# FFN weight units in halves and thirds, ring transfers that wait for their own bytes only, and new planning numbers, in an eight-core decoder step

## The chip, the cores and the metric

The kernel runs on all eight NeuronCores of one Trainium2 chip. Every core runs the same program on its own data: one prompt of 2048 tokens and four decode samples. The metric is the device time of the slowest core, in microseconds. Most executions of one kernel agree within a few tenths of a per cent, but some fall into a slower state, in which one die (four cores) or both run at a lower granted TensorE clock. A ratio below always compares fast runs with fast runs. The chips differ too: the fast runs of the kernel before had a median of about 2395 us where it was first timed and of 2404 to 2407 us on the later chips that had fast runs. So kernels are compared by their ratio to the kernel before in the same rounds, on the same chip.

## The reference, cut to what matters

```
for layer in range(2):
    x = x + 0.5 * swiglu_ffn(rmsnorm(x, ...), ffn_w_in[layer, 0], ffn_w_out[layer, 0])
    x = x + mixer(rmsnorm(x, ...))          # gated linear attention, then dilated window attention
    x = x + 0.5 * swiglu_ffn(rmsnorm(x, ...), ffn_w_in[layer, 1], ffn_w_out[layer, 1])

def swiglu_ffn(x, w_in, w_out):             # w_in 1024 x 5376, w_out 2688 x 1024
    g, u = jnp.split(x @ w_in, 2, axis=-1)
    return (jax.nn.silu(g) * u) @ w_out
```

Four FFNs make up most of the matrix work. Their weights are too large to stay on the core, so they are streamed from HBM once for each of four tiles of 512 tokens. The 32 sample tokens of a core share the loads of tile 0.

## The kernel before: the parts that matter here

The program is written by a small list scheduler. Tiles are Python generators that yield operations. The scheduler plans a start time for every operation from a cost model, and so fixes, before the run, the order of each engine's instructions and the semaphores between them. The plan decides nothing but order. Two tiles are in flight at a time, each with its own ring of weight buffers (12288 bf16 per partition).

```
class Sched:
    DMA_BW = 330e3        # planned rate, bytes of the float32 source per us
    DMA_LAT = 2.2         # planned time from a transfer's end to its landing
    ...
def ffn_units(f):
    for j in range(NF):                                   # 21 units: columns j of g and of u
        add_unit("fi%d" % f, j, wfi[f * NF + j], 2048)
    for m in range(8):                                    # 8 units: 128 output columns
        add_unit("fo%d" % f, m, wfo[f * 8 + m], 2688)

def weights(slot):                                        # one for each ring, issues on POOL
    for k, u in enumerate(order[slot]):
        # ... lo, hi: the next place in the ring; over: units whose bytes it covers
        yield need(lambda over=over: all(o.left == 0 for _, _, o in over))
        yield O(PL, (lambda e: e.dma_start(out=dst, in_=u.src)),
                writes=[u.key] + [o.key for _, _, o in over], cost=1.0, ...)

# in ffn(): a unit is waited for and released as a whole
u = yield from use(T, "fi%d" % f, j)
yield mm(g,  [(v[:, kt, 0:128],   T.h[:, kt, :]) for kt in range(8)], hks(T) + [u.key], ...)
yield mm(up, [(v[:, kt, 128:256], T.h[:, kt, :]) for kt in range(8)], hks(T) + [u.key], ...)
u.left -= 1
```

A load "writes" its own key and the key of every old unit that it covers. If it covers only a part of an old unit, the next load, which covers the rest, finds the first load as the last writer of that key. POOL then waits until the first load has landed before it issues the next, although the two share no byte. The loads narrow float32 to bfloat16 on the way, so 1 GB/s written is 2 GB/s read.

Of the kernel before, what the change touches and what calls it, by code (L numbers as in the profile page):

```python
# [24 lines left out]
class Sched:  # L25



    DMA_BW = 330e3
    DMA_LAT = 2.2  # L30

    def __init__(self, nc):
        self.nc = nc
# [277 lines left out]
def build():  # L311
# [128 lines left out]
    for t in range(4):  # L440
        def add_unit(kind, i, src, n, users=0, t=t):
            u = Unit(src, n, users or (1 if t else 2), (t, kind, i))
            u.kind = kind
            units[(t, kind, i)] = u
            order[t % 2].append(u)

        def ffn_units(f):
            for j in range(NF):
                add_unit("fi%d" % f, j, wfi[f * NF + j], 2048)
            for m in range(8):  # L450
                add_unit("fo%d" % f, m, wfo[f * 8 + m], 2688)
                if (t, f) == (3, 3) and m % 2 == 0:

                    order[0].append(order[1].pop())
        ffn_units(0)
        for gi, kind in enumerate(("v", "qk", "r", "o")):
            for i in range(4):
                add_unit(kind, i, wgl[gi * 4 + i], 2048)
            if t == 0 and kind == "qk":
                for s in range(4):  # L460
                    src = st_in[s * 4:(s + 1) * 4].rearrange("h p d -> p h d")
                    add_unit("S0", s, src, 2048, 1)
                    add_unit("S0b", s, None, 1024, 1)
        ffn_units(1)
        for i in range(2):
            add_unit("kv", i, wkv[i], 2048)
        ffn_units(2)
        for i in range(3):
            add_unit("wq", i, wqd[i], 2048)
        if t == 0:  # L470
            for s in range(4):
                add_unit("ck", s, ck[s], 3328, 1)
                add_unit("cv", s, cv[s], 3328, 1)
        for i in range(4):
            add_unit("wo", i, wod[i], 1536)
        ffn_units(3)
# [1 line left out]


    LEAD = 24 * 2048  # L480
    NWS = 8


    first = {(0, "fi0", 1): [("x", "b0", 5)]}
    for k in range(4):
        first[(1, "fi0", k)] = [units[(0, "fi0", 12 + 2 * k)].key]

    def weights(slot):
        ring = rings[slot]
        live = []  # L490
        off = 0
        yield need(lambda: S.lastw.get(("x", "b0", 7)) is not None)
        for k, u in enumerate(order[slot]):
            if off + u.n > RING or u.kind == "ck":
                off = 0
            lo, hi = off, off + u.n
            off = hi
            over = [(a, b, o) for (a, b, o) in live if a < hi and b > lo]
            yield need(lambda over=over: all(o.left == 0 for _, _, o in over))
            live = [x for x in live if x not in over] + [(lo, hi, u)] + [(a, lo, o) for a, b, o in over if a < lo] \  # L500
                + [(hi, b, o) for a, b, o in over if b > hi]
            u.ap = ring[:, lo:hi]
            if u.uid in first:
                yield need(lambda: all(k in S.lastw for k in first[u.uid]))
            dst = u.ap
            if u.kind == "S0":
                dst = dst.bitcast(F32).rearrange("p (h d) -> p h d", h=4)
            if u.src is None:
                u.keys = [u.key] + [o.key for _, _, o in over]
                u.ready = True  # L510
                continue
            yield O(PL, (lambda e, u=u, dst=dst: e.dma_start(out=dst, in_=u.src)),  # L512
                    first.get(u.uid, []), writes=[u.key] + [o.key for _, _, o in over], cost=1.0, dma="w%d_%d" % (slot, k % NWS), nbytes=u.n * 512)
            u.ready = True

    def use(T, kind, i):
# [124 lines left out]
    def load_x(T, prev):  # L641
        nq = 4 if T.n == 512 else 1
        for q in range(nq):
            ms = range(q * 8 // nq, (q + 1) * 8 // nq)
            if prev is not None:
                yield need(lambda: all(("y", prev.nm, m) in done for m in ms))
            if T.t == 1:
                after = units[(0, "fi0", 3 + 2 * q)]
                yield need(lambda: after.ready)
            w = len(ms) * T.n  # L650
            src = xp[T.t] if T.n == 512 else xs
            yield O(SP, (lambda e, q=q, w=w, src=src, ms=ms: e.dma_start(
                out=T.x[:, ms[0]:ms[-1] + 1, :].rearrange("p m n -> p (m n)"), in_=src[:, q * w:(q + 1) * w])),
                [after.key] if T.t == 1 else [], writes=[xk(T, m) for m in ms], cost=0.1, dma="x%s_%d" % (T.b, q), nbytes=w * 512)
        for m in range(8):
            yield from square(T, m)
# [66 lines left out]
    def hks(T):  # L723
        return [hk(T, m) for m in range(8)]
# [7 lines left out]
    def ffn(T, f, last):  # L732
# [12 lines left out]
            done.add(("act", T.nm, f, j))  # L745

        for j in range(NF):
            u = yield from use(T, "fi%d" % f, j)
            v = u.ap.rearrange("p (kt c) -> p kt c", kt=8)
            if n == 512:  # L750
                bs = yield from get_banks(2)
                g, up = PS[bs[0]], PS[bs[1]]
            else:
                bs = yield from get_banks(1)
                g, up = PS[bs[0]][:, 0:n], PS[bs[0]][:, n:2 * n]
            if j == 0 and n == 512:
                yield from mmh(T, (g, up), lambda kt, z: v[:, kt, z * 128:(z + 1) * 128], [u.key], bs, n)
            else:
                hn = T.hn
                yield need(lambda: ("h", T.nm, hn, 7) in done)  # L760
                yield mm(g, [(v[:, kt, 0:128], T.h[:, kt, :]) for kt in range(8)], hks(T) + [u.key], bs[0], n)
                yield mm(up, [(v[:, kt, 128:256], T.h[:, kt, :]) for kt in range(8)], hks(T) + [u.key], bs[-1], n)
            u.left -= 1
            TH.spawn(post(j, bs, g, up), -3, T.rank)
        yield need(lambda: all(("act", T.nm, f, j) in done for j in range(14)))

# [3 lines left out]
            yield from tail(T, m, last)  # L770

        for m in range(8):
            u = yield from use(T, "fo%d" % f, m)
            v = u.ap.rearrange("p (kt c) -> p kt c", kt=NF)
            (b,) = yield from get_banks(1)
            for q in range(3):
                js = range(7 * q, 7 * q + 7)
                yield need(lambda: all(("act", T.nm, f, j) in done for j in js))
                yield mm(PS[b][:, 0:n], [(v[:, j, :], T.act[:, j, :]) for j in js], [rk(T, ("act", j)) for j in js] + [u.key], b, n,
                         start=(q == 0), stop=(q == 2))  # L780
            u.left -= 1
            TH.spawn(evac(m, b), -4, T.rank)

    def tail(T, m, last):
# [223 lines left out]
    def gla_s(T):  # L1008
# [86 lines left out]
        for s in range(4):  # L1095
# [1 line left out]
            us, ub = (yield from use(T, "S0", s)), (yield from use(T, "S0b", s))  # L1097
            S0 = us.ap.bitcast(F32).rearrange("p (h w) -> p h w", h=4)
            S0b = ub.ap.rearrange("p (h w) -> p h w", h=4)
            yield copy(ACT, S0b, S0, 1024, [us.key], ub.keys)  # L1100
            (b,) = yield from get_banks(1)
            po = PS[b][:, 0:64].rearrange("p (m n) -> p m n", m=8)

            def fo(e, c8=c8, po=po, S0b=S0b):
# [3 lines left out]
                        e.matmul(po[:, hd * 2 + f, :], lhsT=vv[:, hd * 256 + f * 128:hd * 256 + (f + 1) * 128], rhs=am[:, hd, c8], start=True, stop=False)  # L1108
                        ins = e.matmul(po[:, hd * 2 + f, :], lhsT=S0b[:, hd, f * 128:(f + 1) * 128], rhs=qT[:, hd, c8], start=False, stop=True)
                return ins  # L1110
            yield O(PE, fo, [gk, ub.key] + gv, [("ps", b)], c_mm(16, 60))
            yield copy(ACT, oT[:, :, c8], po, 64, [("ps", b)], [rk(T, "go")])
            put(b)
            yield O(DVE, (lambda e, s=s: e.tensor_scalar(out=kms, in0=ktok, scalar1=CF[0:32, A_SQ + s:A_SQ + s + 1], scalar2=None, op0=ALU.mult)),
# [197 lines left out]
    def attention(T):  # L1312
# [24 lines left out]
        def block(g, qsl, kbs, slot):  # L1337
# [16 lines left out]
            keys = []  # L1354
            for kb in kbs:
                keys += [(kb[3][0][0], kb[3][0][1], a) for a in range(2)]
            yield O(PE, fs, keys + [rk(T, ("qt", 2 * g + a)) for a in range(2)], [("ps", b) for b in bs], c_mm(nb * 4, 64) * 1.5)
            for hp in range(2):
                yield act(P[:, hp * w:(hp + 1) * w], PS[bs[hp]][:, 0:w], AF.Exp, w, [("ps", bs[hp])], pk, scale=0.125)
                put(bs[hp])  # L1360
# [34 lines left out]
        def block2(r4, slot):  # L1395
# [9 lines left out]
            def fs(e):  # L1405
                ins = None
                for rr in range(4):
# [5 lines left out]
                                           rhs=T.QT[hp * 64:hp * 64 + 64, 4 + jj, sl_(r, 32, 16)], start=True, stop=True)  # L1413
                return ins
            yield O(PE, fs, [("KT", z, a) for z in range(t + 1) for a in range(2)] + [rk(T, ("qt", 4 + a)) for a in range(2)],
                    [("ps", b) for b in bs], c_mm(16, 32) * 1.2)
            for hp in range(2):
                yield act(P[0:nk, hp * 256:(hp + 1) * 256], PS[bs[hp]][0:nk, 0:256], AF.Exp, 256, [("ps", bs[hp])], pk, scale=0.125)
                put(bs[hp])
# [6 lines left out]
            def fp(e):  # L1426
# [12 lines left out]
                        ins = e.matmul(PS[b][hp * 64:hp * 64 + 64, 256:512], lhsT=CB[kr, B_ONE:B_ONE + 64],  # L1439
                                       rhs=P[kr, hp * 256:hp * 256 + 256], start=False, stop=(ki == len(krs) - 1), skip_group_check=True)  # L1440
                return ins
            yield O(PE, fp, pk + ["CB"] + [("Vg2", z) for z in range(t + 1)], [("ps", b)], c_mm(16, 32) * 1.2 + c_mm(1, 256))
            yield from evac(2, b, o, d, None, r4)

        def worker(slot, mine):
# [34 lines left out]
    def attention_s(T):  # L1480
        for s in range(4):
# [10 lines left out]
            def fs(e, s=s, sv=sv, nv=nv, K3=K3):  # L1492
# [9 lines left out]
                        ins = e.matmul(nv[hp][:, jj, :, :], lhsT=KTs[hp * 64:hp * 64 + 64, jj, :],  # L1502
                                       rhs=T.QT[hp * 64:hp * 64 + 64, jj:6:2, 8 * s:8 * s + 8], start=True, stop=True)
                return ins
            yield O(PE, fs, [uk.key] + [("KTs", a) for a in range(2)] + [rk(T, ("qt", c)) for c in range(6)], [("ps", b) for b in bs], c_mm(56, 40))
            ids = yield from T.pool.get("P", 3, 3)
            kk = [T.pool.key(i) for i in ids]
            P = T.R[:, 1024:1120].rearrange("p (a w) -> p a w", a=2)
# [15 lines left out]
            def fp(e, b=b, ov=ov, P4=P4, P24=P24, V3=V3):  # L1524
# [14 lines left out]
                        e.matmul(ov[hp * 64:hp * 64 + 64, jj, :, :], lhsT=Vsn[0:32, j * 64:(j + 1) * 64], rhs=P24[:, hp, jj, :, :], start=False, stop=False, skip_group_check=True)  # L1539
                    ins = e.matmul(PS[b][hp * 64:hp * 64 + 64, 64:112], lhsT=CB[0:32, B_ONE:B_ONE + 64], rhs=P2[:, hp, :], start=False, stop=True, skip_group_check=True)  # L1540
                return ins
            yield O(PE, fp, [uv.key, "Vsn", "CB", rk(T, "P")], [("ps", b)], c_mm(60, 40))
            uk.left -= 1
            uv.left -= 1
            for jj in range(2):
# [60 lines left out]
def make_in_maps(inp, ncores=8):  # L1606
# [10 lines left out]
        return w.reshape(k, 128, -1).transpose(1, 0, 2)  # L1617

    win = f(inp["ffn_w_in"]).reshape(4, 8, 128, 2, NF, 128)
    wfi = win.transpose(0, 4, 2, 1, 3, 5).reshape(4 * NF, 128, 2048)  # L1620
    wfo = f(inp["ffn_w_out"]).reshape(4, NF, 128, 8, 128).transpose(0, 3, 2, 1, 4).reshape(32, 128, NF * 128)
    gi = f(inp["gla_w_in"])[0]
    gq, gk, gv, glr, gr = gi[:, 0:512], gi[:, 512:1024], gi[:, 1024:2048], gi[:, 2048:2064], gi[:, 2064:3088]
# [57 lines left out]
```

## Time and profile before

The median of its three fast runs was 2394.71 us. In the table, "steps behind DMAs" is worked out from the trace: the time between the starts of two successive matmuls, less the median for that form, where it is over 0.1 us and a DMA ended the wait. "DMA busy" is the sum of a core's packet durations divided by 16 engines. "Saturated rate" is what a core's DMAs wrote in those bins of 2 us in which the engines were over 95% busy. Both are means over eight cores.

| before | value |
|---|---|
| PE busy, slowest core | 2294.8 of 2393.6 us |
| steps behind DMAs | 36 us (22 to 50) |
| half clock | 32 us (20 to 41) |
| DMA busy per engine | 2051 us |
| saturated rate | 182 GB/s written |

The waits view of the kernel before (who waited, for whom: us in total, times, longest us):

```profile
POOL ring L512 <- DMA ring<-wfo: 176.1, 30, 12.7
POOL ring L512 <- DMA ring<-wfi: 155.0, 40, 9.6
...
PE pst L616 <- DMA ring<-wfo: 18.3, 14, 5.0
PE pst L616 <- DMA ring<-wfi: 17.5, 16, 2.6
```

POOL stood for 487 us behind landings of other ring loads (the sum over all weights), which looks like much to win. PE stood for only some 36 us behind the same loads.

One group of the page's fifth part says which matmuls those are (line, engine, operation, what it writes and reads, shapes, count; busy us, mean ns of one; idle us before it, and what ended most of that). `hsb` is the input of the 32 sample tokens:

```profile
L616 PE MATMUL pst<-hsb,ring 128*128 128x32 bf16 x1536 | 53.1, 176 | 27.2 <-DMA ring<-wfi 15.1
```

So 15.1 of the 17.5 us behind the first matrix stand before matmuls of the sample tokens, not of the tiles of 512.

Two pieces of the chain of waits in a dense stretch of the kernel before (start us, length us, what):

```profile
1161.32 10.74 PE pst L616 x49
...
1172.11 10.74 PE pst L616 x49
```

49 matmuls of 512 columns in 10.79 us are 220 ns each. Where weights arrive in time there is little left to win.

### The profile page before, as it was taken

Reading aid. Unit: us, or ns where it says so; the run is one execution under the profiler, and the core shown is the slowest. Engines: PE = TensorE matmul, PEld = TensorE weight load, DVE = VectorE, ACT = ScalarE, POOL = GpSimd, SP = SyncE. Lnnn points to the kernel's source line nnn. Section 1 sums busy time; section 2 is a strip of 40 time slices with the busy share of each in tenths; the row PEclk is TensorE's granted clock in tenths of the full one; section 3 lists DMA queues with packets and bytes.
Section 4 is the critical chain, followed back from the end, with each engine's and each line's share of the span. In section 5 each row is a group of like instructions: output and inputs, shape, how many; then the busy total and the mean of one; then the engine's idle time right before and its main releaser. Section 6 shows DMA issues by size and latency. Waiting matters only on the chain.

```text
span 2393.6 us, 42356 instructions; the slowest of 8 cores (2364.1 to 2393.6 us)
## 1 busy us (share of the span) xinstructions
PE 2294.8 (96%) x14404; PEld 1125.5 (47%) x14660; DVE 1220.4 (51%) x2180; ACT 1172.9 (49%) x2316; POOL 317.8 (13%) x598
## 2 busy tenths in 40 slices
PE   5999999999999989999999999999999999999999
PEld 2445544554444445445444445445444444544444
DVE  4534564455633566446553254654664355654742
ACT  4534655564553365455453245545655334644541
POOL 1111111101111111111111111111111111011110
PEclk9999999999999999999999999999999999999999
DMA  9997697768987988897989988888899889679894
GB/s 177 157 146 138 140 156 128 132 116 144 161 143 131 172 144 153 140 171 135 176 161 171 172 155 150 133 143 148 143 158 171 153 149 173 109 128 169 159 173 91
DMA packets 101362, 357.11 MB, mean 149 GB/s; under 512 B 12528, under 2 KB 17440, under 8 KB 101024
## 3 DMA queue, kind: packets, MB, share of 16 engines
q0 software_dynamic: 84032, 326.13, 80.7%
q1 hardware_dynamic: 17120, 28.25, 3.8%
q8 instruction: 122, 2.00, 0.3%
q14 instruction: 88, 0.72, 0.1%
HBM read 662.94 MB, written 15.40 MB: 283 GB/s over the span
## 4 chain that ended last, share of the span: by engine, by line
PE 79%; DMA 17%; issue 2%; DVE 1%; ACT 1%; POOL 0%; SPq 0%; POOLq 0%; DVEq 0%; ACTq 0%
PE pst L616 75%; DMA ring<-wfi 8%; DMA ring<-wfo 6%; DMA ring<-cv 1%; DMA ring<-wod 1%; DMA x<-xp 1%; PE pst L1411 1%; ACT pb L621 0%; DMA ring<-wkv 0%; PE pst L1350 0%; DMA ring<-wqd 0%; PE pst L1372 0%; DVE pb L629 0%; PE pst L971 0%; POOL ring L512 0%
## 5 line engine op out<-in xcount | busy, mean ns | idle before, releaser
L616 PE MATMUL pst<-h,ring 128*128 128x512 bf16 x5982 | 1369.7, 381 | 17.9 <-DVE h L632 3.5
L616 PEld LDWEIGHTS pst<-h,ring 128*128 128x128 bf16 x6144 | 589.5, 98 | 705.0 <-issue 36.8
L616 PE MATMUL pst<-r,ring 128*128 128x512 bf16 x3052 | 698.3, 380 | 13.9 <-DMA ring<-wfo 7.8
L621 ACT ACTIVATE pb<-pb 128x512 f32<-128x512 f32 x856 | 535.0, 629 | 71.1 <-DVE pb L824 12.5
L621 ACT ACTIVATE pb<-pst 128x512 f32<-128x512 f32 (+1 forms) x472 | 279.0, 595 | 468.4 <-PE pst L616 460.5
L629 DVE TENSOR_TENSOR pb<-pb,pst 128x512 f32<-128x512 f32 x368 | 251.8, 685 | 476.3 <-ACT pb L621 472.9
L616 PEld LDWEIGHTS pst<-r,ring 128*128 128x128 bf16 x3136 | 302.7, 98 | 367.4 <-issue 14.5
L512 POOL DMA_DIRECT2D ring<-wfi x336 | 178.1, 532 | 1057.2 <-PE pst L616 819.0
L621 ACT ACTIVATE h<-x 128x512 bf16<-128x512 f32 x192 | 118.9, 626 | 342.6 <-DVE x L632 232.2
L629 DVE TENSOR_TENSOR r<-pb,pst 128x512 bf16<-128x512 f32 x336 | 230.2, 686 | 45.0 <-DVE pb L629 36.8
L632 DVE SCALAR_TENSOR_TENSOR x<-pst,x 128x512 f32<-128x512 f32 x128 | 88.2, 689 | 201.2 <-PE pst L616 194.3
L632 DVE SCALAR_TENSOR_TENSOR h<-x,CF,pb 128x512 bf16<-128x512 f32 x224 | 150.8, 745 | 20.6 <-ACT pb L621 20.3
L512 POOL DMA_DIRECT2D ring<-wfo x128 | 67.8, 530 | 624.1 <-PE pst L616 375.3
L629 DVE TENSOR_TENSOR pb<-pb,h 128x512 f32<-128x512 f32 x120 | 82.6, 689 | 45.5 <-ACT h L621 43.5
L621 ACT ACTIVATE spb<-pst 128x32 f32<-128x32 f32 (+2 forms) x111 | 21.6, 198 | 118.9 <-PE pst L616 117.5
L616 PE MATMUL pst<-hsb,ring 128*128 128x32 bf16 x1536 | 53.1, 176 | 27.2 <-DMA ring<-wfi 15.1
L616 PEld LDWEIGHTS pst<-hsb,ring 128*128 128x128 bf16 x1536 | 50.1, 96 | 55.3 <-issue 41.7
L616 PE MATMUL pst<-ring,h 128*128 128x256 bf16 x640 | 73.6, 273 | 0.1
L616 PEld LDWEIGHTS pst<-ring,h 128*128 128x128 bf16 x640 | 61.6, 98 | 11.3 <-issue 2.7
L625 ACT COPY r<-pst 128x512 f32<-128x512 f32 (+3 forms) x104 | 50.7, 488 | 26.3 <-PE pst L1439 12.0
L512 POOL DMA_DIRECT2D ring<-wgl x64 | 33.9, 531 | 219.9 <-PE pst L616 143.2
L629 DVE TENSOR_TENSOR x<-x,pst 128x512 f32<-128x512 f32 x64 | 43.8, 686 | 27.4 <-PE pst L616 27.2
(150 smaller groups left out, 1093.2 us busy)
## 6 DMA issues: line engine op xcount, KB each, us to landing
ring<-wfi POOLq DMA_DIRECT2D x336, 512.0 KB, 8.6
ring<-wfo POOLq DMA_DIRECT2D x128, 672.0 KB, 8.3
ring<-wgl POOLq DMA_DIRECT2D x64, 512.0 KB, 7.0
x<-xp SPq DMA_DIRECT2D x16, 512.0 KB, 10.6
y_p<-x SPq DMA_DIRECT2D x32, 256.0 KB, 7.4
ring<-wqd POOLq DMA_DIRECT2D x12, 512.0 KB, 10.0
ring<-wod POOLq DMA_DIRECT2D x16, 384.0 KB, 7.5
ring<-wkv POOLq DMA_DIRECT2D x8, 512.0 KB, 8.6
```

The lines of the kernel that those rows point to most:

```text
L512: yield O(PL, (lambda e, u=u, dst=dst: e.dma_start(out=dst, in_=u.src)), first.get(u.uid, []), writes=[u.key] + [o.key for _, _, o in over ...
L616: ins = e.matmul(out, lhsT=l, rhs=r, start=(start and i == 0), stop=(stop and i == last), skip_group_check=skip)
L621: return O(ACT, lambda e: e.activation(out=out, in_=in_, func=func, scale=scale, bias=bias), reads, writes, c_act(n))
L625: return O(ACT, lambda e: e.copy(out=out, in_=in_), reads, writes, c_act(n))
L629: return O(DVE, lambda e: e.tensor_tensor(out=out, in0=a, in1=b, op=op), reads, writes, c_dve(n, rate))
L632: return O(DVE, lambda e: e.scalar_tensor_tensor(out=out, in0=a, scalar=s, in1=b, op0=op0, op1=op1), reads, writes, c_dve(n))
L1411: ins = e.matmul(PS[bs[hp]][0:nk, rr * 64 + jj * 32:rr * 64 + jj * 32 + 32], lhsT=KT[hp * 64:hp * 64 + 64, jj, sl_(r, nk, 16)], rhs=T.QT[h ...
```

## The change

The intent is to release ring bytes earlier and to need fewer bytes before a matmul group can start. A unit of the first FFN matrix becomes two halves (g and u), one of the second becomes three thirds of the contraction. Each part is loaded, waited for and released by itself. A load waits only for the last writer and the readers of the bytes that it covers. The cost model gets new numbers.

```
-    DMA_BW = 330e3
-    DMA_LAT = 2.2
+    DMA_BW = 315e3
+    DMA_LAT = 3.2
 ...
             for j in range(NF):
-                add_unit("fi%d" % f, j, wfi[f * NF + j], 2048)
+                for z in range(2):
+                    add_unit("fi%d" % f, (j, z), wfi[f * NF + j][:, z * 1024:(z + 1) * 1024], 1024)
             for m in range(8):
-                add_unit("fo%d" % f, m, wfo[f * 8 + m], 2688)
+                for q in range(3):
+                    add_unit("fo%d" % f, (m, q), wfo[f * 8 + m][:, q * 896:(q + 1) * 896], 896)
 ...
+            S.readers[u.key] = [t for _, _, o in over for t in [S.lastw[o.key]] + S.readers[o.key]]
 ...
-                    first.get(u.uid, []), writes=[u.key + ...over keys...], cost=1.0, ...)
+                    first.get(u.uid, []), writes=[u.key], cost=0.6, ...)
 ...
-            u = yield from use(T, "fi%d" % f, j)         # then PSUM banks, two groups, one release
+            # PSUM banks first, then for each half: use, 8 matmuls, release
 ...                                                      # likewise for the thirds
-            yield O(PE, fo, [gk, ub.key] + gv, [("ps", b)], c_mm(16, 60))
+            yield O(PE, fo, [gk, ub.key] + gv, [("ps", b)], 1.68)
 ...                                                      # five more TensorE costs of small groups
```

The cuts leave out index arithmetic, a changed host layout of the first matrix (so that a half is contiguous in each row), and 16 instead of 8 semaphores for each ring.

More of the change, by code (lines that the diff above doesn't have):

```diff
@@ L448, in ffn_units @@
             for j in range(NF):
-                add_unit("fi%d" % f, j, wfi[f * NF + j], 2048)
+                for z in range(2):
+                    add_unit("fi%d" % f, (j, z), wfi[f * NF + j][:, z * 1024:(z + 1) * 1024], 1024)
             for m in range(8):
-                add_unit("fo%d" % f, m, wfo[f * 8 + m], 2688)
+                for q in range(3):
+                    add_unit("fo%d" % f, (m, q), wfo[f * 8 + m][:, q * 896:(q + 1) * 896], 896)
                 if (t, f) == (3, 3) and m % 2 == 0:
-                    order[0].append(order[1].pop())
+                    order[0] += order[1][-3:]
+                    del order[1][-3:]
         ffn_units(0)
@@ L480, in build @@
     LEAD = 24 * 2048
-    NWS = 8
-    first = {(0, "fi0", 1): [("x", "b0", 5)]}
+    NWS = 16
+    first = {(0, "fi0", (1, 0)): [("x", "b0", 5)]}
     for k in range(4):
-        first[(1, "fi0", k)] = [units[(0, "fi0", 12 + 2 * k)].key]
+        first[(1, "fi0", (k, 0))] = [units[(0, "fi0", (12 + 2 * k, 1))].key]
     def weights(slot):
@@ L507, in weights @@
                 dst = dst.bitcast(F32).rearrange("p (h d) -> p h d", h=4)
+            S.readers[u.key] = [t for _, _, o in over for t in [S.lastw[o.key]] + S.readers[o.key]]
             if u.src is None:
-                u.keys = [u.key] + [o.key for _, _, o in over]
                 u.ready = True
@@ L512, in weights @@
             yield O(PL, (lambda e, u=u, dst=dst: e.dma_start(out=dst, in_=u.src)),
-                    first.get(u.uid, []), writes=[u.key] + [o.key for _, _, o in over], cost=1.0, dma="w%d_%d" % (slot, k % NWS), nbytes=u.n * 512)
+                    first.get(u.uid, []), writes=[u.key], cost=0.6, dma="w%d_%d" % (slot, k % NWS), nbytes=u.n * 512)
             u.ready = True
@@ L647, in load_x @@
             if T.t == 1:
-                after = units[(0, "fi0", 3 + 2 * q)]
+                after = units[(0, "fi0", (3 + 2 * q, 0))]
                 yield need(lambda: after.ready)
@@ L747, in ffn @@
         for j in range(NF):
-            u = yield from use(T, "fi%d" % f, j)
-            v = u.ap.rearrange("p (kt c) -> p kt c", kt=8)
+            us = []
+            if j == 0 and n == 512:
+                for z in range(2):
+                    us.append((yield from use(T, "fi%d" % f, (j, z))))
             if n == 512:
@@ L756, in ffn @@
             if j == 0 and n == 512:
-                yield from mmh(T, (g, up), lambda kt, z: v[:, kt, z * 128:(z + 1) * 128], [u.key], bs, n)
+                yield from mmh(T, (g, up), lambda kt, z: us[z].ap[:, kt * 128:kt * 128 + 128], [u.key for u in us], bs, n)
+                for u in us:
+                    u.left -= 1
             else:
@@ L760, in ffn @@
                 yield need(lambda: ("h", T.nm, hn, 7) in done)
-                yield mm(g, [(v[:, kt, 0:128], T.h[:, kt, :]) for kt in range(8)], hks(T) + [u.key], bs[0], n)
-                yield mm(up, [(v[:, kt, 128:256], T.h[:, kt, :]) for kt in range(8)], hks(T) + [u.key], bs[-1], n)
-            u.left -= 1
+                for z, dst in ((0, g), (1, up)):
+                    u = yield from use(T, "fi%d" % f, (j, z))
+                    v = u.ap.rearrange("p (kt c) -> p kt c", kt=8)
+                    yield mm(dst, [(v[:, kt, :], T.h[:, kt, :]) for kt in range(8)], hks(T) + [u.key], bs[min(z, len(bs) - 1)], n)
+                    u.left -= 1
             TH.spawn(post(j, bs, g, up), -3, T.rank)
@@ L772, in ffn @@
         for m in range(8):
-            u = yield from use(T, "fo%d" % f, m)
-            v = u.ap.rearrange("p (kt c) -> p kt c", kt=NF)
             (b,) = yield from get_banks(1)
             for q in range(3):
+                u = yield from use(T, "fo%d" % f, (m, q))
+                v = u.ap.rearrange("p (kt c) -> p kt c", kt=7)
                 js = range(7 * q, 7 * q + 7)
                 yield need(lambda: all(("act", T.nm, f, j) in done for j in js))
-                yield mm(PS[b][:, 0:n], [(v[:, j, :], T.act[:, j, :]) for j in js], [rk(T, ("act", j)) for j in js] + [u.key], b, n,
+                yield mm(PS[b][:, 0:n], [(v[:, j % 7, :], T.act[:, j, :]) for j in js], [rk(T, ("act", j)) for j in js] + [u.key], b, n,
                          start=(q == 0), stop=(q == 2))
-            u.left -= 1
+                u.left -= 1
             TH.spawn(evac(m, b), -4, T.rank)
@@ L1099, in gla_s @@
             S0b = ub.ap.rearrange("p (h w) -> p h w", h=4)
-            yield copy(ACT, S0b, S0, 1024, [us.key], ub.keys)
+            yield copy(ACT, S0b, S0, 1024, [us.key], [ub.key])
             (b,) = yield from get_banks(1)
@@ L1356, in block @@
                 keys += [(kb[3][0][0], kb[3][0][1], a) for a in range(2)]
-            yield O(PE, fs, keys + [rk(T, ("qt", 2 * g + a)) for a in range(2)], [("ps", b) for b in bs], c_mm(nb * 4, 64) * 1.5)
+            yield O(PE, fs, keys + [rk(T, ("qt", 2 * g + a)) for a in range(2)], [("ps", b) for b in bs], nb * 4 * 0.056)
             for hp in range(2):
@@ L1415, in block2 @@
             yield O(PE, fs, [("KT", z, a) for z in range(t + 1) for a in range(2)] + [rk(T, ("qt", 4 + a)) for a in range(2)],
-                    [("ps", b) for b in bs], c_mm(16, 32) * 1.2)
+                    [("ps", b) for b in bs], 16 * (0.029 + nk * 0.00027))
             for hp in range(2):
@@ L1441, in fp @@
                 return ins
-            yield O(PE, fp, pk + ["CB"] + [("Vg2", z) for z in range(t + 1)], [("ps", b)], c_mm(16, 32) * 1.2 + c_mm(1, 256))
+            yield O(PE, fp, pk + ["CB"] + [("Vg2", z) for z in range(t + 1)], [("ps", b)], 0.48)
             yield from evac(2, b, o, d, None, r4)
@@ L1504, in fs @@
                 return ins
-            yield O(PE, fs, [uk.key] + [("KTs", a) for a in range(2)] + [rk(T, ("qt", c)) for c in range(6)], [("ps", b) for b in bs], c_mm(56, 40))
+            yield O(PE, fs, [uk.key] + [("KTs", a) for a in range(2)] + [rk(T, ("qt", c)) for c in range(6)], [("ps", b) for b in bs], 0.84)
             ids = yield from T.pool.get("P", 3, 3)
@@ L1541, in fp @@
                 return ins
-            yield O(PE, fp, [uv.key, "Vsn", "CB", rk(T, "P")], [("ps", b)], c_mm(60, 40))
+            yield O(PE, fp, [uv.key, "Vsn", "CB", rk(T, "P")], [("ps", b)], 1.4)
             uk.left -= 1
@@ L1619, in make_in_maps @@
     win = f(inp["ffn_w_in"]).reshape(4, 8, 128, 2, NF, 128)
-    wfi = win.transpose(0, 4, 2, 1, 3, 5).reshape(4 * NF, 128, 2048)
+    wfi = win.transpose(0, 4, 2, 3, 1, 5).reshape(4 * NF, 128, 2048)
     wfo = f(inp["ffn_w_out"]).reshape(4, NF, 128, 8, 128).transpose(0, 3, 2, 1, 4).reshape(32, 128, NF * 128)
```

## The prediction

> **What bounds the kernel now.** TensorE: 2294.8 us busy of 2393.6 (page, part 1). In dense stretches the chain of waits shows 49 matmuls of 512 columns per 10.79 us; the trace's matmul starts are 216 ns apart (median). Summing each form's median step gives 2208 us, plus about 53 for 256 records missing on the slowest core: about 2260 us of matmul stream. At most about 130 us can be won: about 25 at start and end, about 47 in steps where PE waited for a ring DMA (the waits view shows only 18.3 for wfo and 17.5 for wfi, since part hides under the modelled matmul length), about 28 behind DVE (norms), some 25 in short "issue" gaps. Over the cores the steps behind ring DMAs sum to 22 to 50 us; the cores with most (1, 2, 6) are slow, 2387 to 2394 us, those with least (3, 5) take 2364 and 2368. The change aims at this part.
>
> **Why PE waits.** Traced back to the late DMA's issue on core 2: half the stalled time, POOL issued only after PE had released the whole old unit; 30%, after POOL had waited for another DMA to land (waits view: POOL behind wfo 176, wfi 155, wgl 71 us and so on, some 490 in all). Then 8 to 9 us pass to landing. The worst stall, 5.2 us near 1365, follows a run of landing waits.
>
> **What the change does.** (1) wfi in halves, wfo in thirds: a buffer is released 1.7 us (8 matmuls) to 3 us (14) earlier, and a unit's first matmuls need only its half or third. (2) A transfer waits only for the last writer and readers of its bytes, not for its neighbour's landing: most of the 490 us should go. (3) The list scheduler gets slower, later DMA and other PE costs, so PE's order changes; I cannot cost that.
>
> **What it adds.** 592 more DMAs. POOL: 0.53 us each, +314 us on an engine 13% busy: harmless. DMA engines: uncontended packets of 2048, 4096, 5376 bytes took about 172, 322, 416 ns, so some 22 ns fixed each. Two 2048 for one 4096: +7%; three 1792 (estimate 153 ns) for one 5376: +10%; with more semaphore packets (21 ns) about 115 us per engine, share 85% to 89%. The Trainium skill (DMA: Bandwidth & Descriptors, "Why small descriptors are slow") names a fixed cost per packet; this trace agrees. Slices already saturate the engines (share 1.0 from 20 to 100 us); there finer packets cost something. Matmuls stay the same[...].
>
> **Sum.** On the slow cores 50 to 70% of the ring stalls go (-25 to -35 us), a few us return from DMA overhead, and better order and start give a little: about -34 us. Predicted time 2360 us, range 2330 to 2395. Chances: faster by over 2% 0.29, within 2% 0.67, slower 0.04.
>
> **What would show it.** POOL's waits on ring landings fall from 490 to under 150 us; PE steps behind ring DMAs to 15 to 25 us; wfi 256 KB x672, wfo 224 KB x384; DMA share up 3 to 5 points; PE busy about unchanged, share 97%; the spread of the cores shrinks.
>
> **What would make it wrong.** DMA engines or HBM, not release times, set the stalls (they stay, share near 1.0); or the changed order removes norm stalls too (under 2330), or makes new ones at tile changes.

## More of the kernel before

"Half clock" is the time between a core's first and last matmul for which the trace's clock records grant half the clock.

Lines of the page (engines' busy time; DMA busy in tenths over 40 slices of the span; packets; queue; issues with KB each and the median us from issue to landing), kernel before, slowest core:

```profile
span 2393.6 us, 42356 instructions; the slowest of 8 cores (2364.1 to 2393.6 us)
PE 2294.8 (96%) x14404; PEld 1125.5 (47%) x14660; DVE 1220.4 (51%) x2180; ACT 1172.9 (49%) x2316; POOL 317.8 (13%) x598
...
DMA  9997697768987988897989988888899889679894
...
DMA packets 101362, 357.11 MB, mean 149 GB/s; under 512 B 12528, under 2 KB 17440, under 8 KB 101024
...
q0 software_dynamic: 84032, 326.13, 80.7%
...
ring<-wfi POOLq DMA_DIRECT2D x336, 512.0 KB, 8.6
ring<-wfo POOLq DMA_DIRECT2D x128, 672.0 KB, 8.3
```

TensorE is busy 96% of the time, but the DMA queue of the weights is also busy 80.7%, and many slices are at 90% or more.

## The result, and the profile after

The changed kernel was slower. In the first series its fast runs took 1.013 times those of the kernel before (95% interval 1.010 to 1.016), but four of its six runs there were slow. Repeated on another chip as `after_again`, it took 1.0139 (1.0107 to 1.0171): the fast runs' median was 2438 us against 2404. At a threshold of 2% that is "the same", but it is clear of noise, above the predicted range, and of the wrong sign.

A ratio here is made from the fast runs of both kernels in the same rounds. It is not quite the ratio of the medians or of the plain means: the two ways differ by up to 0.0014 (after_lat6).

The first profile of the changed kernel fell into the slow state (one die at clock 0.953), so the lines below are those of the repeat. They are the same lines of the page as above, for the slowest core of `after_again`:

```profile
span 2436.6 us, 44935 instructions; the slowest of 8 cores (2395.8 to 2436.6 us)
PE 2331.6 (96%) x14660; PEld 1131.7 (46%) x14660; DVE 1220.0 (50%) x2180; ACT 1170.6 (48%) x2316; POOL 629.4 (26%) x1190
...
DMA  9998898889999989997999989899899999699894
...
DMA packets 186626, 357.29 MB, mean 147 GB/s; under 512 B 22000, under 2 KB 76064, under 8 KB 186272
...
q0 software_dynamic: 169280, 326.17, 89.9%
...
ring<-wfi POOLq DMA_DIRECT2D x672, 256.0 KB, 10.3
ring<-wfo POOLq DMA_DIRECT2D x384, 224.0 KB, 7.2
```

The same bytes now take twice the packets on the weight queue, and it is busy 89.9% where it was 80.7%. A load of half the size takes longer from issue to landing (10.3 us against 8.6), one of a third only a little less (7.2 against 8.3).

The waits view of the same run:

```profile
POOL ring L516 <- DMA ring<-wfi: 20.1, 5, 8.0
...
PE pst L620 <- DMA ring<-wfi: 36.2, 30, 3.0
PE pst L620 <- DMA ring<-wfo: 13.7, 7, 5.1
```

POOL's waits for landings went from 487 to 21 us, as I had predicted. PE's waits for the loads did not fall with them: those for the first matrix rose. The group of the sample tokens again:

```profile
L620 PE MATMUL pst<-hsb,ring 128*128 128x32 bf16 x1536 | 64.8, 177 | 47.0 <-DMA ring<-wfi 36.2
```

All 36.2 us stand before matmuls of the sample tokens. Over the eight cores, the steps behind DMAs before sample matmuls rose from 29 to 43 us, and those before the tiles of 512 fell from 7 to 4. A sample matmul of 32 columns starts 25 ns after the one before it (median), so half a unit gives PE only 0.2 us of that work. The change did what it was meant to do for the large tiles, where little was to be won.

What waits cost beyond themselves is in the clock. Three stretches of the same core (us; busy us of PE, PEld, DVE, ACT and POOL with instructions; granted clock; DMA share; GB/s written); the last one lies inside the second row's stretch:

```profile
1370.00:1390.00 20.00, 20.00 (x94) 8.92 (x91) 4.75 (x7) 1.89 (x3) 5.30 (x11) 1.00 1.04 171
1390.00:1410.00 20.00, 10.73 (x35) 3.81 (x35) 6.23 (x9) 4.39 (x8) 1.58 (x3) 0.77 1.05 170
...
1394.00:1401.00 7.00, 4.02 (x10) 1.46 (x11) 0.00 (x0) 0.00 (x0) 0.27 (x1) 0.51 1.02 166
```

In the first stretch PE ran dense. In the second it waited 5.1 us for a load of the second matrix while the DMA engines were saturated (share 1.05). 2.2 us into that wait the clock went to half, for 6.8 us, and the matmuls after the load ran at half speed until then (some 430 ns apart, where they had been 216). Per core, means over eight cores:

| | before | changed (`after_again`) |
|---|---|---|
| steps behind DMAs, us | 36 (22 to 50) | 47 (38 to 62) |
| steps behind DVE or ACT, us | 26 | 35 |
| half clock, us (at most half of it is lost) | 32 | 55 |
| DMA busy per engine, us | 2051 | 2282 |
| saturated rate, GB/s written | 182 | 168 |

The mean core took 2380.7 us in the profile of the kernel before and 2413.2 in that of the changed one. The differences in the first two rows, and half of the third, sum to 11 + 9 + 11.5, or about 32 us, which is about that gap. The two profiles come from different chips, so this is a rough check. On the chip of `after_again` itself the mean core of the fast runs went from 2390 to 2421 us, or 31 us.

### The profile page after: what moved, and what is told of

Its sections match the earlier page's. It is cut to its first block, busy times and chain, and to the rows that moved or that the text cites. A ratio compares the mean times of both kernels' runs of the same rounds, so it can differ in the third digit from the quotient of the medians.

```text
span 2487.4 us, 44935 instructions; the slowest of 8 cores (2402.7 to 2487.4 us)
## 1 busy us (share of the span) xinstructions
PE 2398.2 (96%) x14660; PEld 1152.0 (46%) x14660; DVE 1220.3 (49%) x2180; ACT 1168.4 (47%) x2316; POOL 629.4 (25%) x1190
## 4 chain that ended last, share of the span: by engine, by line
PE 89%; DMA 8%; issue 1%; ACT 0%; DVE 0%; POOL 0%; SPq 0%; POOLq 0%; DVEq 0%; ACTq 0%
PE pst L620 85%; DMA ring<-wfi 4%; DMA ring<-wfo 3%; DMA x<-xp 1%; PE pst L1421 1%; DMA ring<-wqd 0%; DMA ring<-ck 0%; PE pst L1360 0%; PE pst L1382 0%; PE pst L981 0%; PE pst L998 0%; PE pst L999 0%; ACT pb L625 0%; PE pst L1444 0%; PE pst L1386 0%
## 5 line engine op out<-in xcount | busy, mean ns | idle before, releaser
L620 PE MATMUL pst<-h,ring 128*128 128x512 bf16 x6144 | 1456.5, 391 | 4.5 <-DVE h L636 3.0
L620 PEld LDWEIGHTS pst<-h,ring 128*128 128x128 bf16 x6144 | 596.8, 100 | 721.1 <-issue 164.9
L620 PE MATMUL pst<-r,ring 128*128 128x512 bf16 x3136 | 742.3, 388 | 7.6 <-DMA ring<-wfo 7.5
L516 POOL DMA_DIRECT2D ring<-wfi x672 | 354.9, 530 | 1026.8 <-PE pst L620 954.5
L516 POOL DMA_DIRECT2D ring<-wfo x384 | 202.8, 528 | 525.9 <-PE pst L620 442.5
L620 PEld LDWEIGHTS pst<-hsb,ring 128*128 128x128 bf16 x1536 | 62.8, 98 | 77.0 <-issue 62.9
L620 PE MATMUL pst<-hsb,ring 128*128 128x32 bf16 x1536 | 65.1, 178 | 29.7 <-DMA ring<-wfi 23.8
L620 PE MATMUL pst<-ring,h 128*128 128x256 bf16 x640 | 80.8, 287 | 0.0
L625 ACT ACTIVATE h<-pst 128x512 bf16<-128x512 f32 (+4 forms) x96 | 46.6, 512 | 35.3 <-PE pst L1421 17.8
L629 ACT COPY r<-pst 128x512 f32<-128x512 f32 (+3 forms) x104 | 51.1, 492 | 19.3 <-PE pst L1449 10.3
```

Source lines behind the costliest of these rows:

```text
L516: yield O(PL, (lambda e, u=u, dst=dst: e.dma_start(out=dst, in_=u.src)), first.get(u.uid, []), writes=[u.key], cost=0.6, dma="w%d_%d" % (s ...
L620: ins = e.matmul(out, lhsT=l, rhs=r, start=(start and i == 0), stop=(stop and i == last), skip_group_check=skip)
L625: return O(ACT, lambda e: e.activation(out=out, in_=in_, func=func, scale=scale, bias=bias), reads, writes, c_act(n))
L629: return O(ACT, lambda e: e.copy(out=out, in_=in_), reads, writes, c_act(n))
```

## The experiments

The theories at the start were these.

- **Packet theory.** Smaller transfers cost the DMA engines more, the weights come later, and that costs what release gains.
- **Order theory.** The new cost numbers and units give the scheduler a worse order of PE's work.
- **Deeper queue.** With no landing waits, more loads are in flight and an urgent one stands behind others.

To tell order from DMA work, some kernels hold the order of TensorE, VectorE and ScalarE as another kernel had it. The sequence of all operations and of all grants of banks and buffers is recorded and followed, and only the weight loads are placed anew. All runs gave correct results. The edits below are shortened.

### First series: a disturbed chip

On this chip die 0 had a low clock in every run. The numbers are means over the four cores of die 1, in the runs in which its clock was above 0.984.

**split_dma_only**: the kernel before, each FFN load issued as two or three transfers by columns, waited for and released as a whole.

```
-    yield O(PL, lambda e: e.dma_start(out=dst, in_=u.src), ...)
+    def load(e):                       # parts = 2 (first matrix) or 3 (second)
+        for p in range(parts - 1):
+            e.dma_start(out=dst[:, p*w:(p+1)*w], in_=u.src[:, p*w:(p+1)*w]).then_inc(sem, 16)
+        return e.dma_start(out=dst[:, (parts-1)*w:], in_=u.src[:, (parts-1)*w:])
```

> The kernel before, instruction for instruction, but each FFN weight load is issued as two (first matrix) or three (second matrix) transfers that are waited for and released together, so no unit is freed or ready earlier. Packet theory (smaller transfers cost the DMA engines more): DMA busy per engine rises from about 2050 us to about 2260, rate while saturated falls from about 182 to about 170 GB/s, and the time is 20 to 50 us above before. Order theory (the list scheduler's new order is what costs): same as before, within 6 us.

Measured: 2426 us against 2379 for the kernel before on the same die. The whole cost is there, without any change of order.

**bytes_only_same_order**: whole units, byte-wise waits, order held as before.

```
+            S.readers[u.key] = [t for _, _, o in over for t in [S.lastw[o.key]] + S.readers[o.key]]
-                    writes=[u.key] + [o.key for _, _, o in over], ...
+                    writes=[u.key], ...
```

> The kernel before with whole units and the order of its TensorE, VectorE and ScalarE work held as before; only ring transfers wait for readers of their bytes alone. If the landing waits mattered as I predicted: 5 to 20 us faster than before, with the DMA waits of POOL gone (490 us to under 100). Rival, deeper queue (more loads in flight, an urgent one stands behind those of the other ring): 5 to 20 us slower, and loads take longer from issue to landing.

Measured: 2377 against 2379 us. Neither expectation holds. POOL's landing waits vanished and the time did not move. The waits of an engine that is not the bottleneck had cost nothing.

**full_dma_same_order**: the change's whole DMA side, with the old cost numbers, order held as before.

> All of the change's DMA side (halves and thirds, each freed by itself, byte-wise waits) with the order of TensorE, VectorE and ScalarE work held as before (24 of 8874 steps had to move). Order theory: faster than before by 10 to 35 us, as I predicted for the DMA side. Packet theory: 5 to 35 us slower than before, close to the changed kernel.

Measured: 2384 against 2379 us, against 2408 to 2410 for the changed kernel on undisturbed dies in its own series. Given the old order, the DMA side nearly broke even, at the lowest end of what the packet theory gave. Neither theory alone explains the change.

**new_costs_only**: the kernel before with the new numbers of the cost model and nothing else.

```
-    DMA_BW = 330e3
-    DMA_LAT = 2.2
+    DMA_BW = 315e3
+    DMA_LAT = 3.2
 ... # and the six TensorE costs of the change
```

> The kernel before with the change's new numbers in the scheduler's cost model only (DMA rate and latency, six TensorE costs); whole units, old waits. Order theory: most of the loss, 15 to 35 us slower than before, and more time at half clock. Packet theory: within 8 us of before.

Measured: 2364 against 2379 us. The order theory had the wrong sign: for whole units the new numbers are a gain, and steps behind DMAs are 9 us per core where the kernel before had 36 on another chip.

### Second series: ratios

**split_by_partition**: as split_dma_only, but cut by partitions, so that packets keep their number and length.

```
-            e.dma_start(out=dst[:, p*w:(p+1)*w], in_=u.src[:, p*w:(p+1)*w])
+            e.dma_start(out=dst[a:b], in_=u.src[a:b])    # 64+64, or 48+48+32 partitions
```

> As split_dma_only (same program order, 592 more transfers), but a load is cut by partitions (64+64, or 48+48+32) and not by columns, so there are as many packets, and as long ones, as before. If the cost of the split is per packet: within 10 us of before, DMA busy back near 2060 us per engine. If it is per transfer (issue on POOL, semaphore, queue): still 30 to 50 us slower than before, as split_dma_only was on the undisturbed die (mean of its cores 2426.0 against 2379.0 us).

Measured: 1.0015 (0.9991 to 1.0038), DMA busy 2084 us. The repeat of the cut by columns, **split_dma_only_2**, was:

> Again split_dma_only, for a ratio in the fast state. Packet theory: 1.015 to 1.025 of before (2426.0 against 2379.0 us, 1.020, on the undisturbed die).

Measured: 1.0291 (1.0255 to 1.0327), above its range; DMA busy 2240 us, steps behind DMAs 90 us. Packets and queue of the two, cut by partitions first:

```profile
DMA packets 110839, 357.19 MB, mean 148 GB/s; under 512 B 22000, under 2 KB 26912, under 8 KB 110496
...
q0 software_dynamic: 93504, 326.17, 82.5%
```

```profile
DMA packets 186615, 357.19 MB, mean 144 GB/s; under 512 B 22000, under 2 KB 76064, under 8 KB 186272
...
q0 software_dynamic: 169280, 326.17, 87.4%
```

Both kernels issue 592 transfers more than the kernel before and run the same instructions in the same order. Only the one whose packets are shorter is slower. The cost comes with the shorter packets, not with the number of transfers: 592 more issues on POOL and their semaphores cost at most 0.4% (the end of the interval). A cut by columns also breaks up each row that is read. Whether the number of packets or that access costs was not separated.

**full_old_costs**: the changed kernel with all the old cost numbers, free to order.

> The changed kernel with the old numbers in the scheduler's cost model, free to order. full_dma_same_order was 5 us above before on the undisturbed die, the changed kernel about 30. If the new cost numbers ruin the order where units are small: 2375 to 2390 us mean of an undisturbed die. If it is the units themselves that give the scheduler a worse order whatever the numbers: 2400 to 2415.

Measured: 1.0292 (1.0262 to 1.0323); die means 2461 and 2455 us. That is beyond both ranges, on the side of "the units themselves". PE's waits for the loads, from the waits view of its slowest core:

```profile
PE pst L620 <- DMA ring<-wfi: 66.7, 46, 4.6
PE pst L620 <- DMA ring<-wfo: 24.8, 24, 4.9
```

Steps behind DMAs are 106 us per core here, against 34 to 45 with nearly the same loads in the order of the kernel before. So with small units the scheduler's own order is worse, and the new cost numbers had mended half of that.

**whole_bytes_new_costs**: the change without the split.

> The change without the split: byte-wise waits and new cost numbers, whole units. If the split is what turns the change into a loss, and the two other parts add up: 2355 to 2365 us mean of an undisturbed die (before 2379, new_costs_only 2364, bytes_only_same_order 2377), faster than before and 45 us below the changed kernel. If byte-wise waits hurt under the new order: 2370 or more.

Measured: 0.9860 (0.9838 to 0.9882), die means 2364 and 2362 us, as expected. This kernel beats both: the median of its fast runs is 2372 us where the kernel before had 2404. Its span and PE's waits:

```profile
span 2370.0 us, 42650 instructions; the slowest of 8 cores (2354.8 to 2370.0 us)
...
PE pst L617 <- DMA ring<-wfi: 14.5, 6, 5.7
PE pst L617 <- DMA ring<-wfo: 14.0, 6, 9.5
```

**new_dma_model_only**: the kernel before with only the planned DMA rate and latency changed.

> The kernel before with only DMA rate and latency of the cost model changed, not the six TensorE costs. If the gain of new_costs_only (15 us on the undisturbed die) comes from the slower, later DMA that the model plans with: 2360 to 2369 us mean of an undisturbed die, PE steps behind ring DMAs 4 to 15 us per core. If it comes from the TensorE costs: 2375 or more.

Measured: 0.9881 (0.9840 to 0.9921), steps behind DMAs 14 us (7 to 23). The gain of the cost numbers is in these two lines. The six TensorE costs add nothing that these runs can tell.

### Third series: what is wrong with the order of small units

The idea (margin theory) was this. Whole units saturate at 182 GB/s written, 364 GB/s of source; the split ones at about 169, or 338. A plan made at 315 has about 15% of slack in the first case and 7% in the second.

**after_again**: the changed kernel, for reference on this chip.

> The changed kernel unaltered, on the same chip as the next three, because only two of its runs were in the fast state. All theories: 1.010 to 1.017 of before in the fast state, PE steps behind ring DMAs 35 to 53 us per core, half-clock time near 60 us per core.

Measured: 1.0139, as quoted above; half clock 55 us, steps behind DMAs 38 to 62 us.

**after_bw300**: `DMA_BW = 300e3` in the changed kernel.

> The changed kernel with the planned DMA rate of the scheduler at 300 instead of 315 GB/s of source bytes. Margin theory (the split lowered the saturated rate from about 364 to about 338 GB/s of source bytes, so a plan made at 315 has only 7% of slack, where whole units had 14%): slack of 13%, PE steps behind ring DMAs fall from about 44 to 15 to 25 us per core, and the time to about 2375 to 2395 us, near before. Rival (the order is worse because of how units are taken, not of the planned rate): within 8 us of the changed kernel.

Measured: 1.0050 (1.0007 to 1.0092, from two fast runs), steps behind DMAs 35 us (25 to 50). These steps are of a profile in the slow state; its undisturbed die alone had 38. The time moved about two thirds of the way, the stalls less than expected. A slower plan helps, but not by the amount that the margin theory gave.

**after_use_first**: the changed kernel, a tile waits for its unit before it takes PSUM banks.

```
-            bs = yield from get_banks(2)
-            ...
-            u = yield from use(T, "fi%d" % f, (j, z))
+            u = yield from use(T, "fi%d" % f, (j, 0))
+            bs = yield from get_banks(2)
```

> The changed kernel, but a tile waits for its weight unit before it takes PSUM banks, as the kernel before did (the change had turned this round). If tiles that hold banks while their unit is on its way spoil the order: 10 to 25 us faster than the changed kernel. Margin theory: within 8 us of it.

Measured: 1.0134 (1.0097 to 1.0171). The banks are not the cause.

**whole_bytes_bw300**: `DMA_BW = 300e3` in whole_bytes_new_costs.

> The best kernel so far (whole units, byte-wise waits, new costs; 0.986 of before) with the planned DMA rate at 300. Whole units already have slack at 315, so margin theory expects little: 0.980 to 0.988 of before, PE steps behind ring DMAs under 20 us per core (they were 19 to 31). More than 0.99 would say that a plan can also be too slow.

Measured: 0.9875 (0.9850 to 0.9900). Steps behind DMAs fell to 15 us, but steps behind DVE and ACT rose from 20 to 33.

### Fourth series: order, landing time, units

**full_dma_same_order_2**: the first held-order kernel again, on a good chip.

> The same kernel as full_dma_same_order, again, to have it against before with all eight cores and beside the next. Order theory (small units are cheap when the order of before is held): 0.998 to 1.006 of before. Units theory (small units cost as much in any order): 1.010 or more.

Measured: 1.0004 (0.9984 to 1.0023). The order theory's range holds: the same small loads, in the old order, cost nothing net.

**after_best_order**: the changed kernel with the order held as in whole_bytes_new_costs.

> The changed kernel with the order of TensorE, VectorE and ScalarE held as in whole_bytes_new_costs (0.986 of before); 53 of some 8900 steps had to move. In its plan 81 of 1164 units are used within 2 us of landing, 289 in the changed kernel. Order theory: 0.986 to 0.996 of before, PE steps behind ring DMAs 15 to 35 us per core. Units theory: 1.008 or more.

Measured: 1.0009 (0.9991 to 1.0027), steps behind DMAs 49 us. It lies between the two ranges. The best order is not enough: in it the small units cost 1.5% more than whole ones.

**after_lat6**: `DMA_LAT = 6.0` in the changed kernel.

> The changed kernel with the planned landing 6.0 instead of 3.2 us after a transfer's end, free order. If just-in-time plans meet late landings: PE steps behind ring DMAs fall from about 47 to under 30 us per core, time 1.000 to 1.008 of before. If the landing time in the plan is not what matters: 1.010 to 1.018, as the changed kernel.

Measured: 0.9995 (0.9976 to 1.0013), just below its range. Steps behind DMAs are 33 us (just over the expected 30), those behind DVE and ACT 27, half clock 35. One number in the plan takes back the whole loss of 1.4%. PE's waits on its slowest core, to set beside 36.2 and 13.7 us of the changed kernel:

```profile
PE pst L620 <- DMA ring<-wfi: 22.3, 24, 2.5
...
PE pst L620 <- DMA ring<-wfo: 10.9, 7, 5.1
```

**whole_lat6**: the same number in whole_bytes_new_costs.

> whole_bytes_new_costs with the planned landing at 6.0 us. If a later planned landing helps there too: 0.978 to 0.984 of before. Otherwise 0.985 to 0.990; the plan itself is 12 us longer.

Measured: 0.9878 (0.9862 to 0.9894). It does not help where units are whole.

**whole_bytes_split_loads**: whole_bytes_new_costs in its own program order, each FFN load cut by columns and released as a whole.

> whole_bytes_new_costs (0.986 of before), same program order, but each FFN load issued as two or three transfers by columns and released as a whole. Packet cost in the best order: 1.000 to 1.010 of before. As after_best_order (same order, but each part released by itself) is at 1.0009, a value above it is what earlier release gives back; a value near 0.99 would say that packets cost little here and the separate units themselves do.

Measured: 0.9950 (0.9916 to 0.9984), DMA busy 2240 us against 2095 for whole_bytes_new_costs. It lies below the expected range: the cut costs 0.9% in this order, where it cost 2.9% in the order and with the landing waits of the kernel before.

### The sum

| step | kernel | ratio to before | this step |
|---|---|---|---|
| byte-wise waits and new cost numbers, whole units | whole_bytes_new_costs | 0.9860 | -1.4% |
| FFN loads cut by columns, released as a whole | whole_bytes_split_loads | 0.9950 | +0.9% |
| each part released by itself, order still held | after_best_order | 1.0009 | +0.6% |
| the scheduler's own order for these units: the change | after_again | 1.0139 | +1.3% |

The step from the second to the third row is small. Its two intervals (0.9916 to 0.9984, and 0.9991 to 1.0027) just miss each other, and 53 steps of the order had to move. It also takes in the rest of the change's DMA side (a unit for each part, 16 semaphores, the host layout). What it shows is that releasing parts earlier gained nothing there. In the order of before, cut loads with landing waits cost 2.9%, and with byte-wise waits and early release together 0.0%. Which of the two takes that back was not separated.

The last row is not a matter of weights. Between the profiles of after_best_order and after_again, steps behind DMAs are 49 and 47 us per core, but steps behind DVE or ACT go from 23 to 35 and half clock from 44 to 55.

## Why the prediction was wrong, point by point

- **"At most about 130 us can be won"; TensorE bounds the kernel.** No run contradicts it as an upper limit. But I read 80.7% on the weight queue as headroom. It is a second limit within some 20% of the first.
- **Landing waits of POOL fall from 490 us to under 150.** Right: 487 to 21 us. That they matter was wrong: without them, and with nothing else changed, the mean of the undisturbed die moved by 2 us. This is the reasoning that failed first. I traced 30% of PE's stalled time to loads that POOL had issued late behind a landing, without asking whether the DMA engines would have served them earlier. They were saturated in about two thirds of all bins of 2 us.
- **"50 to 70% of the ring stalls go (-25 to -35 us)".** This step failed. Steps behind DMAs went from 36 to 47 us per core. With order held as before they stayed at 34 and 45 us in two profiles. My gain of 1.7 to 3 us for each release was reckoned in matmuls of 512 columns; but 29 of the 36 us stood before sample matmuls, and that part rose to 43.
- **"About 115 us per engine ... a few us return".** The mechanism was right, the size was not. DMA busy rose by 232 us. My 22 ns per packet came from uncontended packets. The new medians confirm it (173 ns for 2048 bytes, 154 for 1792). On average, load included, a 4096-byte packet of the weight queue took 388 ns before, and two of 2048 bytes took 2 x 226 = 452 in the changed kernel. The loss in time was 0.9 to 2.9% by itself.
- **"I cannot cost [the order]".** I set it to about nothing. It was +1.3% for the small units. In the kernel with whole units the same two DMA numbers were -1.2%. The largest gain of the whole change and one of its two largest losses were in the step that I did not cost.
- **Share of PE busy, transfers.** PE's share stayed at 96% (97% forecast), and 672 and 384 transfers of 256 and 224 KB came as expected. DMA share rose by 9 points on the weight queue, not 3 to 5. The spread of the cores did not shrink: 29 us before, 41 after.
- **"DMA engines or HBM, not release times, set the stalls"** was named as what would make me wrong. It is most of the answer, and the order is the rest. I gave the two together too small a chance.
- **What I had left out: the clock.** Half clock goes with stalls: in the 8 us before an episode at half clock, some step between matmul starts was over 1 us in 36 of 59 episodes before and in 68 of 83 after, but only before about a tenth of moments drawn at random. Time at half clock rose from 32 to 55 us per core, up to 11.5 us of the loss.

The Trainium skill could have warned me. Perfetto Trace Analysis, section "DMA Optimizations", recommends splitting transfers so that some start sooner, on a condition: "If DMA engines are generally idle". Here they were busy 2051 of about 2381 us, so the condition was not met, and split_dma_only_2 at 1.0291 agrees with the condition. DMA: Bandwidth & Descriptors, section "Why small descriptors are slow (HBM only)", names the fixed cost per packet; split_by_partition at 1.0015 beside it fits that: shorter packets cost, more transfers do not.

Open: why the scheduler's free order for small units is worse. With the old numbers (full_old_costs) it stalls more behind loads, 106 us; with the change's numbers it waits longer behind DVE and ACT and is longer at half clock. A slower plan took back two thirds of the loss (after_bw300, 1.005), a later planned landing all of it (after_lat6, 0.9995). In the plans themselves 289 of the 1164 units of the changed kernel are used within 2 us of their planned landing, and 288 in after_lat6, counted by running the scheduler. So not fewer units are just in time; they are just in time for a later landing. That the 2.8 us more are what shields them is argued, not shown. Nor does this count foretell the stalls: after_best_order has only 81 such units, and its steps behind DMAs are 49 us.

## What to carry to other kernels

Before cutting transfers, look at the busy share of the DMA engines and at the packets: here, with the engines busy 2051 of about 2381 us, a cut that shortened packets cost 0.9 to 2.9% by itself, and one that kept their length (by partitions) cost 0.15%, which is within its noise. Look also at which matmuls wait: here most of the waiting was before the small matmuls of the 32 sample tokens, for which an earlier half unit buys almost nothing. Waits of the engine that issues DMAs are no gain in themselves; trace on to whether the transfers would have run sooner. If a static scheduler orders the program, its planned DMA rate and landing time are tuning parameters like any other: here two of them were worth 1.2% with no other change, and after the cut another value of one of them was worth 1.4%.

## What the Trainium skill lacked or had wrong

- DMA: Bandwidth & Descriptors, "Why small descriptors are slow (HBM only)", puts the fixed cost at about 3 cycles a packet, 27% at 256 bytes; for 2048 against 4096 bytes written that would be an estimated 2% (two times 64 + 3 beats against 128 + 3). In these narrowing loads two 2048-byte packets took 7% longer than one of 4096 by medians (2 x 173 against 324 ns) and 17% longer on average under load (2 x 226 against 388 ns, means of the weight queue).
- The same page, "Specifications", calls 512 bytes enough for line rate. Here going from 4096 and 5376 bytes to 2048 and 1792 lowered the saturated rate from 182 to 168 GB/s written; between split_by_partition and split_dma_only_2, which differ in the cut alone, it is 179 and 171.
- TensorE: Matmul & The Clock Gate, "HAM oscillation — how this bites in real kernels", says that no gap between matmuls should exceed about 3.4 us. The episodes at half clock here do last 3.4 us or a multiple of it (3.4, 6.8, 10.2, once 13.7), but most followed shorter gaps: leaving out each core's start and end, in 51 of the 59 episodes of the kernel before and 66 of the 83 of the changed one, the longest step between matmul starts in the 8 us before was under 3.4 us.
- No page gives the cost of cutting a load by partitions. DMA: Bandwidth & Descriptors, "Rules for kernel authors", only advises against it, since the parts share the same DMA engines. Here it was nearly free: 592 more transfers at a ratio of 1.0015 (0.9991 to 1.0038).
